# Prologue without GpSimd subtractions, half of the modulation as single columns on TensorE, and a 128-row bias product

## The chip, the cores and the metric

The kernel runs on one core of a Trainium2 chip. The metric is the device time of one execution in microseconds (us), lower is better; the median of three runs before the change is 1759.72 us (1759.67 to 1759.94). Engines are called as the profile calls them: PE (TensorE, the matmuls), PEld (its weight loads), DVE (VectorE), ACT (ScalarE), POOL (GpSimd) and SP (SyncE, which here only issues DMAs).

## The reference

A decoder block on x of 1024 tokens by 1024 channels, in float32. What matters here is its head and one projection:

```python
mod = silu(c) @ w_ada + b_ada              # one row of 6*1024 values
sh1, sc1, g1, sh2, sc2, g2 = split(mod, 6)
h = rms_norm(x, norm_mix_g) * (1.0 + sc1) + sh1
proj = h @ w_in + b_in                     # glu, q/k, v, o, gates, merge
glu_in, qk_in, v, o_pre, if_pre, merge_pre = split(proj)
# a 31-tap causal convolution with GLU beside a chunked mLSTM over q, k, v;
# both merged by sigmoid gates, then w_out, a residual, and a SwiGLU FFN
```

Only sh1 and sc1 (2 x 1024 values, from the first 2048 columns of `w_ada`) are needed before the first projection; the value projection is `v = h @ w_in[:, V] + b_in[V]`.

## The kernel before

Each product of float32 matrices is made of three float32r products: hi x hi, hi x lo and lo x hi, where hi is the value rounded to float32r (written by ACT) and lo is the rest (a subtraction). So each 128-column block of `w_in` needs a load (`wraw`, L140), a hi copy on ACT (L149) and a lo subtraction (L150); then 96 matmuls of 128x512 (L159) over eight 128-channel slices k.

**The prologue** loads x, normalizes its rows (L229 to L238), transposes them on PE into `xT[k]` (L242, evacuated by ACT at L245 or DVE at L247) and computes the modulation. `w_ada` comes as four groups g of 256 channels; a group's tile `wad` holds [128 rows, 8 slices k, 2 halves, 256], half 0 for the shift and half 1 for the scale, and comes by four DMAs (L197). `mod_cols(g)` multiplies each slice by its value of silu(c) and adds it to `macc` on DVE (L266, L268), both halves in one 128x512 instruction. PE then sums `macc` over the partitions with a column of ones (L270, four products of one column) into a one-buffer PSUM tile `pa`; ACT turns these into two columns of `sh1` (L273) and of the gain `G1` (L274). With them ACT writes `hh[k]`, the hi part of h (L304), and h itself over `xT[k]` (L308), and the difference `hl[k]` is a subtraction (L309), for k = 0 and 1 on POOL and else on DVE. `first_products(g)` (L283) is 24 matmuls of 128x512 for the first two blocks of `w_in` (`wf`), whose lo parts POOL subtracts, as it does for the two blocks that come next (`w_next`, POOL at L150, stored as `wlo`). Rows of small parameters (`rows`, L119) are loaded too and transposed by PE into columns (L126, copied by DVE at L129); the first of these holds the bias that ACT needs for its first sigmoid (L364). The first matmul after the prologue is that of L159 in the block of `w_next`.

**Later**, for each of four heads, the value projection (`v_half`, twice) makes four output tiles; each starts with a bias product (L549) of a [64, 128] tile of ones with `b_two`, a [64, 256] tile that is zero but for row 0 (hi of the bias) and row 32 (lo), and 24 matmuls of 128x256 follow (L552 to L554). These are 32 bias products in all.

**What sets the order.** The kernel is written with a tile framework that schedules instructions with its own model of time; each engine then runs its list strictly in the order so found, and waits where a semaphore isn't there yet. DMAs that SP issues take eight semaphores in turn, and each issue after the eighth waits until the DMA that last used its semaphore has landed. `wraw` has two buffers and `pa` has one.

Of the kernel before, what the change touches and what calls it, by code (L numbers as in the profile page):

```python
# [8 lines left out]
F32 = mybir.dt.float32  # L9
F32R = mybir.dt.float32r  # L10
I32 = mybir.dt.int32
AF = mybir.ActivationFunctionType
OP = mybir.AluOpType
# [4 lines left out]
KT = 8  # L18
# [16 lines left out]
AT = (43, 43, 46, 49, 20, 20, 49, 49, 4, 12, 66, 64)  # L35
SCALE = "vvvvvvva"
EVAC = ("aaaaaaaa", "avaavaav")
ON_POOL = (0, 1)
KX = 6
MACC = 3  # L40
XB = 7
# [8 lines left out]
def hybrid_block(ctx: ExitStack, tc: tile.TileContext, x, c, w_ada, b_ada, norm_mix_g, w_in, b_in,  # L50
                 conv_dw_w, conv_dw_b, conv_ln_g, conv_ln_b, w_conv_pw, b_conv_pw, qk_conv_w,
                 qk_conv_b, mlstm_norm_g, w_out, norm_ffn_g, w_ffn_up, w_ffn_down, final_norm_g, out):
    nc = tc.nc
# [5 lines left out]
    const = ctx.enter_context(tc.tile_pool(name="const", bufs=1))  # L59
# [8 lines left out]
    def ps_a():  # L68
        return ps.tile([128, 512], F32, name="pa", bufs=1)

    def ps_n():
        return ps.tile([128, 512], F32, name="pn", bufs=1)

    def ps_c():
        return ps.tile([128, 512], F32, name="pc", bufs=2)
# [20 lines left out]
    ones_col = const.tile([128, 1], F32, name="ones_col")  # L96
    nc.vector.memset(ones_col, 1.0)
    ones_d = const.tile([128, 128], F32, name="ones_d")
    nc.vector.memset(ones_d, 1.0 / D)
    ones_v = const.tile([64, 128], F32R, name="ones_v")  # L100
    nc.vector.memset(ones_v.bitcast(F32), 1.0)
    ones16 = ones_col[0:16, 0:1].to_broadcast([16, 256])

# [3 lines left out]
    def as_rows(ap, n):  # L107
        return bass.AP(tensor=ap.tensor, offset=ap.offset, ap=[[128, n], [1, 128]])
# [3 lines left out]
    def param_rows(group, plan, t=None):  # L112
        if t is None:
            t = pro.tile([128, 128], F32, name=f"rows{group}")
        if sum(n for _, _, n in plan) < 128:
            nc.vector.memset(t, 0.0)
        at = 0
        for key, ap, n in plan:
            nc.sync.dma_start(t[at:at + n, :], ap)  # L119
            at += n  # L120
        return group, plan, t

    def param_columns(rows):
        group, plan, t = rows
        p = ps_a()
        nc.tensor.transpose(p[:, 0:128], t, ident)  # L126
        n = sum(n for _, _, n in plan)
        col = const.tile([128, n], F32, name=f"col{group}")
        nc.vector.tensor_copy(col, p[:, 0:n])  # L129
        at = 0  # L130
        for key, ap, n in plan:
            cols[key] = col[:, at:at + n]
            at += n
# [40 lines left out]
    hh = [big.tile([128, S], F32R, name=f"hh{k}", tag="xa") for k in range(KT)]  # L174

    G1 = const.tile([128, KT], F32, name="G1")
    sh1 = const.tile([128, KT], F32, name="sh1")

    prologue = ExitStack()
    pro = prologue.enter_context(tc.tile_pool(name="pro", bufs=1, reuse_waits="tile"))  # L180
    rows = pro.tile([128, 8, 128], F32, name="rows", tag="macc", bufs=MACC)
    param_columns(param_rows(1, [("c", as_rows(c, 8), 8)], rows[:, 0]))
    sc_c = const.tile([128, KT], F32, name="sc_c")
    nc.scalar.activation(sc_c, cols["c"], AF.Silu)
    xt = []
    for i in range(4):
        t = pro.tile([128, 2, D], F32, name=f"xt{i}")
        nc.sync.dma_start(t, x2[i * 256:(i + 1) * 256, :].rearrange("(a p) d -> p a d", p=128))
        xt += [t[:, 0, :], t[:, 1, :]]
    wad = []  # L190
# [9 lines left out]

    param_columns(param_rows(6, [("b_ada", as_rows(b_ada, 48), 48), ("mix_g", as_rows(norm_mix_g, 8), 8)], rows[:, 1]))
    load_ada(0)
    WF = nc.gpsimd
    WN = nc.gpsimd
    w_first = []
    for i in range(2):
        w_hi, w_lo = (pro.tile([128, KT, 128], F32R, name=f"wf{i}{j}") for j in range(2))
        w_first.append(load_split(win, 0, KT, GLU_B if i == 0 else 0, w_hi, w_lo, eng=WF))
    load_ada(1)
# [16 lines left out]
    for q in range(2):  # L226
# [12 lines left out]
        for k in range(KT):  # L239
            p = ps_n() if k % 3 == 0 else ps_c()  # L240
            for t in range(4):
                nc.tensor.transpose(p[:, t * 128:(t + 1) * 128], xt[q * 4 + t][:, k * 128:(k + 1) * 128], ident)  # L242
            h = xT[k][:, q * 512:(q + 1) * 512]
# [13 lines left out]

    def mod_cols(g):
        p = ps_a()
        part = lambda t, i: t[:, i // 2, (i % 2) * 128:(i % 2) * 128 + 128]  # L260
        b = mod_b[:, g]
        acc = pro.tile([128, 2, 2, 256], F32, name="macc", tag="macc", bufs=MACC)
        for k in range(KT):
            a = acc[:, 0]
            if k < 1:
                nc.vector.tensor_scalar(a, wad[g][:, k], sc_c[:, k:k + 1], None, op0=OP.mult)  # L266
            else:
                nc.vector.scalar_tensor_tensor(a, wad[g][:, k], sc_c[:, k:k + 1], a, op0=OP.mult, op1=OP.add)  # L268
        for i in range(4):
            nc.tensor.matmul(p[:, i:i + 1], part(acc[:, 0], i), ones_col, start=True, stop=True)  # L270
        for i in range(2):
            k = 2 * g + i
            nc.scalar.activation(sh1[:, k:k + 1], p[:, i:i + 1], AF.Identity, bias=b[:, 0, i:i + 1])  # L273
            nc.scalar.activation(G1[:, k:k + 1], p[:, 2 + i:3 + i], AF.Identity, scale=mix_g[:, g, i:i + 1], bias=b[:, 1, i:i + 1])  # L274
# [11 lines left out]
    hl = []  # L286
    for g in range(4):
        mod_cols(g)
        if g == 2:
            rows = pro.tile([128, 8, 128], F32, name="rows", tag="macc", bufs=MACC)  # L290
            later = [
                param_rows(5, [("b_lo", rows_at(b_in, 0, 48), 48), ("b_hi", rows_at(b_in, MC0, 16), 16)], rows[:, 0]),
                param_rows(3, [("dw0", rows_at(conv_dw_w, 0, 128), 128)], rows[:, 1]),
                param_rows(4, [("dw1", rows_at(conv_dw_w, 128 * 128, 120), 120)], rows[:, 2]),
                param_rows(2, [
                    ("dw_b", as_rows(conv_dw_b, 8), 8), ("ln_g", as_rows(conv_ln_g, 8), 8),
                    ("ln_b", as_rows(conv_ln_b, 8), 8), ("pw_b", as_rows(b_conv_pw, 8), 8),
                    ("qk_b", as_rows(qk_conv_b, 16), 16), ("ml_g", as_rows(mlstm_norm_g, 8), 8),
                    ("ffn_g", as_rows(norm_ffn_g, 8), 8), ("qk_w", as_rows(qk_conv_w, 64), 64)], rows[:, 3])]
            bif = const.tile([128, 8], F32, name="bif")  # L300
            nc.sync.dma_start(bif, bass.AP(tensor=b_in.tensor, offset=b_in.offset + IF0, ap=[[0, 128], [1, 8]]))
        ks = (2 * g, 2 * g + 1)
        for k in ks:
            nc.scalar.activation(hh[k], xT[k], AF.Identity, bias=sh1[:, k:k + 1], scale=G1[:, k:k + 1])  # L304
        for k in ks:
            h = xT[k]
            hl.append(big.tile([128, S], F32R, name=f"hl{k}", tag="xb"))
            nc.scalar.activation(h, h, AF.Identity, bias=sh1[:, k:k + 1], scale=G1[:, k:k + 1])  # L308
            (nc.gpsimd if k in ON_POOL else nc.vector).tensor_sub(hl[k], h, hh[k].bitcast(F32))  # L309
        if g > 0:  # L310
            first_products(g - 1)
    first_products(3)
# [9 lines left out]
    hp = hdp.enter_context(tc.tile_pool(name="hp", bufs=1, side="left", reuse_waits="tile"))  # L322
# [47 lines left out]
    def wblock(col0, busy=PUMP, raw=None):  # L370
        w = load_split(win, 0, KT, col0, raw=raw, eng=WN if raw is not None else None)
        acc = ps_mm()
# [143 lines left out]
    def qkv(h):  # L516
# [4 lines left out]
        nc.gpsimd.memset(vl.bitcast(F32)[:, :, 256:258], 0.0)  # L521

        bcols = slice(V0 + h * 256, V0 + h * 256 + 256)
        b_raw, b_hi, b_two = (hp.tile([64, 256], dt, name=n) for n, dt in (("vb_raw", F32), ("vb_hi", F32R), ("vb_two", F32R)))
        nc.gpsimd.memset(b_raw, 0.0)
        for r in (0, 32):
            nc.sync.dma_start(b_raw[r:r + 1, :], b_in[0:1, bcols])
# [34 lines left out]
        q, k = [], []  # L562
# [318 lines left out]
    p = ps_a()  # L881
# [344 lines left out]
    for gidx, nf in enumerate(groups):  # L1226
# [4 lines left out]
        for t in range(8):  # L1231
# [3 lines left out]
            if gidx < 3:  # L1235
                p = ps_mm()
# [40 lines left out]
```

## Time and profile before

| | |
|---|---|
| times of the three runs | 1759.94, 1759.72, 1759.67 us |
| span of the profiled execution | 1757.5 us; its time outside the span isn't on the page, and the runs' median lies 2.2 us above the span |
| PE busy | 1716.9 us, 98% of the span |
| DVE busy | 1253.3 us, 71% |
| ACT busy | 610.9 us, 35% |
| POOL busy | 72.9 us, 4% |
| first matmul after the prologue (L159) | 67.88 us after the span's start |

The span runs from the first instruction to the last. A group's row gives the sum of its instructions' busy time, the mean of one, and how long the engine sat idle just before them. PE's ends are modelled and its matmuls overlap, so on PE the distance from start to start is what an instruction takes of the time, and not its duration.

### The profile page before, as it was taken

The page shows a single profiled execution, that of the slowest core. Times are in us where ns is not written, and L with a number is a line of the kernel's source. Part 1 is how long each engine was busy: PE and PEld are TensorE (multiplying, and loading weights), DVE is VectorE, ACT ScalarE, POOL GpSimd, SP SyncE. Part 2 cuts the span into 40 slices and gives each one's busy share as a digit, 9 for nine tenths or more (in the row PEclk, how much of TensorE's full clock was granted, in tenths as well). Part 3 has the DMA queues.
Part 4 walks back from the last instruction along what each step waited for, and adds up shares of the span by engine and source line. Part 5 has one row for each costly group of instructions (what it writes and reads, how often), then busy time and mean ns, then how long its engine had stood idle before and what let it go on. Part 6 is the DMA issues. An engine that isn't in the chain of part 4 may idle for free.

```text
span 1757.5 us, 21022 instructions
## 1 busy us (share of the span) xinstructions
PE 1716.9 (98%) x8448; PEld 1436.9 (82%) x8448; DVE 1253.3 (71%) x1652; ACT 610.9 (35%) x791; POOL 72.9 (4%) x121
## 2 busy tenths in 40 slices
PE   5999999999999999999999999999999999999998
PEld 4788888888888888888888788888888888878887
DVE  6888998996689858737689567866666665685243
ACT  6434334322533243223522366423222321232122
POOL 3100001000100000000000000000000000000000
PEclk8999999999999999999999999999999999999999
DMA  9121111111111211224497643322222222653221
GB/s 333 33 60 40 46 60 49 49 60 60 49 37 60 62 46 48 73 60 163 136 374 261 204 156 109 108 84 72 84 84 84 72 85 90 221 168 104 64 89 56
DMA packets 194712, 179.93 MB, mean 102 GB/s; under 512 B 7463, under 2 KB 166711, under 8 KB 194615
## 3 DMA queue, kind: packets, MB, share of 16 engines
q1 hardware_dynamic: 177367, 146.61, 26.8%
q10 hardware_dynamic: 17248, 31.99, 5.0%
q8 instruction: 66, 1.08, 0.3%
q14 instruction: 31, 0.25, 0.0%
HBM read 146.06 MB, written 32.51 MB: 102 GB/s over the span
## 4 chain that ended last, share of the span: by engine, by line
PE 90%; DVE 4%; DMA 3%; issue 1%; ACT 1%; POOL 0%; SPq 0%; POOLq 0%; DVEq 0%; ACTq 0%
PE mm L159 39%; PE mm L1054 5%; PE mm L1055 5%; PE mm L1056 4%; PE mm L552 2%; PE mm L1240 2%; PE mm L1239 2%; PE mm L1241 2%; PE mm L553 2%; PE mm L554 2%; PE pc L1054 1%; DVE macc L268 1%; PE pc L1056 1%; PE pc L1055 1%; PE pa L1056 1%
## 5 line engine op out<-in xcount | busy, mean ns | idle before, releaser
L340 DVE SCALAR_TENSOR_TENSOR cacc<-a,col,cacc 128x1024 f32<-128x1024 f32 x240 | 307.3, 1286 | 4.1 <-ACT cacc L338 1.4
L159 PE MATMUL mm<-hh,whi 128*128 128x512 f32 x864 | 272.8, 392 | 0.8 <-ACT t L364 0.8
L159 PE MATMUL mm<-hl,whi 128*128 128x512 f32 x864 | 271.0, 392 | 0.0
L159 PE MATMUL mm<-hh,wlo 128*128 128x512 f32 x864 | 270.6, 391 | 0.0
L159 PEld LDWEIGHTS mm<-hh,whi 128*128 128x128 f32 x864 | 161.1, 188 | 32.8 <-ACT t L364 1.2
L159 PEld LDWEIGHTS mm<-hh,wlo 128*128 128x128 f32 x864 | 161.3, 188 | 32.3
L159 PEld LDWEIGHTS mm<-hl,whi 128*128 128x128 f32 x864 | 160.5, 188 | 30.9 <-issue 0.2
L149 ACT ACTIVATE whi<-wraw 128x1024 fp32r<-128x1024 f32 x62 | 65.8, 1062 | 228.7 <-PE mm L159 178.5
L150 DVE TENSOR_TENSOR wlo<-wraw,whi 128x1024 fp32r<-128x1024 f32 x60 | 73.2, 1220 | 26.1 <-ACT whi L149 26.0
L552 PE MATMUL mm<-whi,hh 128*128 128x256 f32 x256 | 76.2, 298 | 0.0
L1054 PE MATMUL mm<-Bh,gh 128*128 128x512 f32 (+1 forms) x192 | 71.6, 375 | 1.5 <-ACT gh L994 1.0
L553 PE MATMUL mm<-whi,hl 128*128 128x256 f32 x256 | 72.5, 283 | 0.0
L1055 PE MATMUL mm<-Bl,gh 128*128 128x512 f32 (+1 forms) x192 | 71.5, 373 | 0.6 <-DVE Bl L976 0.6
L554 PE MATMUL mm<-wlo,hh 128*128 128x256 f32 x256 | 71.8, 283 | 0.0
L1056 PE MATMUL mm<-Bh,gl 128*128 128x512 f32 (+1 forms) x192 | 71.2, 372 | 0.0
L505 DVE SCALAR_TENSOR_TENSOR cacc<-qkraw,col,cacc 128x1024 f32<-128x1024 f32 x48 | 61.5, 1280 | 6.7 <-ACT cacc L503 6.0
L1243 DVE TENSOR_TENSOR x<-x,mm 128x1024 f32<-128x1024 f32 x24 | 29.3, 1219 | 51.1 <-PE mm L1241 47.0
L1119 ACT ACTIVATE whi<-wraw 128x512 fp32r<-128x512 f32 (+2 forms) x32 | 25.3, 790 | 110.6 <-PE mm L1241 72.9
L552 PEld LDWEIGHTS mm<-whi,hh 128*128 128x128 f32 x256 | 48.8, 191 | 4.1
L1240 PE MATMUL mm<-fa,wlo 128*128 128x512 f32 x128 | 50.1, 392 | 1.0 <-DVE wlo L1120 0.9
L1239 PE MATMUL mm<-fa,whi 128*128 128x512 f32 x128 | 50.0, 390 | 0.9 <-DVE cu L1082 0.9
L1241 PE MATMUL mm<-fa,whi 128*128 128x512 f32 x128 | 49.9, 390 | 0.0
(442 smaller groups left out, 3898.0 us busy)
## 6 DMA issues: line engine op xcount, KB each, us to landing
wraw<-in_w_in_dram SPq DMA_DIRECT2D x64, 512.0 KB, 4.2
awt<-in_w_ada_dram SPq DMA_DIRECT2D x32, 512.0 KB, 8.1
graw<-in_w_ffn_up_dram SPq DMA_DIRECT2D x24, 512.0 KB, 3.8
uraw<-in_w_ffn_up_dram SPq DMA_DIRECT2D x22, 512.0 KB, 4.7
draw<-in_w_ffn_down_dram SPq DMA_DIRECT2D x22, 512.0 KB, 4.4
act_d<-cg ACTq DMA_DIRECT2D x38, 256.0 KB, 2.2
wad<-in_w_ada_dram SPq DMA_DIRECT2D x16, 512.0 KB, 10.2
wraw<-in_w_out_dram SPq DMA_DIRECT2D x16, 512.0 KB, 4.3
```

The costliest lines, as they stand in the source:

```text
L150: (eng or nc.vector).tensor_sub(lo, raw, hi.bitcast(F32))
L159: nc.tensor.matmul(flat(acc)[:, a:b], lhs[:, k, :], rhs[k][:, a:b], start=(first and k == 0), stop=(last and k == kt - 1))
L340: nc.vector.scalar_tensor_tensor(acc, a[:, j:j + S], dw_col(j, ct), acc, op0=OP.mult, op1=OP.add)
L552: nc.tensor.matmul(o, hh[k][:, ts_], hi[:, k % 4, :], start=False, stop=False)
L553: nc.tensor.matmul(o, hl[k][:, ts_], hi[:, k % 4, :], start=False, stop=False)
L554: nc.tensor.matmul(o, hh[k][:, ts_], lo[:, k % 4, :], start=False, stop=(k == KT - 1))
L1054: nc.tensor.matmul(o, a, rh, start=(k == 0), stop=False)
L1055: nc.tensor.matmul(o, a, rl, start=False, stop=False)
L1056: nc.tensor.matmul(o, b, rh, start=False, stop=(k == 3))
L1239: nc.tensor.matmul(o, hi[:, i, :], his[i][:, a:b], start=(i == 0), stop=False)
L1240: nc.tensor.matmul(o, lo[:, i, :], his[i][:, a:b], start=False, stop=False)
L1241: nc.tensor.matmul(o, hi[:, i, :], los[i][:, a:b], start=False, stop=(i == nf - 1))
```

## The change

Five edits, all but the last in the prologue.

1. The four lo subtractions of weights (`wf`, `w_next`) and those of `hl[0]` and `hl[1]` go from POOL to DVE.
2. h (L308) is made by a DVE instruction with two scalars a partition, instead of by ACT.
3. In `mod_cols` DVE accumulates the shift half alone (128x256). The scale half is left to PE: for each 128 columns and each k a product of one column, with the `wad` slice as weights and the column k of silu(c) moving, 16 in a group, adding up in PSUM. The products with ones go from four in a group to two.
4. `macc` is 256 wide instead of 1024, and `rows` has buffers of its own, so that its loads no longer wait for a `macc` buffer.
5. The bias product of the value projection has 128 rows instead of 64; the rows added are zero in `b_two`.

```diff
-WF = nc.gpsimd
-WN = nc.gpsimd
+WF = nc.vector
+WN = nc.vector
...
-        acc = pro.tile([128, 2, 2, 256], F32, name="macc", tag="macc", bufs=MACC)
+        acc = pro.tile([128, 256], F32, name="macc", tag="macc", bufs=MACC)
+        for i in range(2):
+            for k in range(KT):
+                nc.tensor.matmul(p[:, 2 + i:3 + i], wad[g][:, k, 1, i * 128:(i + 1) * 128], sc_c[:, k:k + 1],
+                                 start=(k == 0), stop=(k == KT - 1))
         for k in range(KT):
-            a = acc[:, 0]
             if k < 1:
-                nc.vector.tensor_scalar(a, wad[g][:, k], sc_c[:, k:k + 1], None, op0=OP.mult)
+                nc.vector.tensor_scalar(acc, wad[g][:, k, 0], sc_c[:, k:k + 1], None, op0=OP.mult)
             else:
-                nc.vector.scalar_tensor_tensor(a, wad[g][:, k], sc_c[:, k:k + 1], a, op0=OP.mult, op1=OP.add)
-        for i in range(4):
-            nc.tensor.matmul(p[:, i:i + 1], part(acc[:, 0], i), ones_col, start=True, stop=True)
+                nc.vector.scalar_tensor_tensor(acc, wad[g][:, k, 0], sc_c[:, k:k + 1], acc, op0=OP.mult, op1=OP.add)
+        for i in range(2):
+            nc.tensor.matmul(p[:, i:i + 1], acc[:, i * 128:(i + 1) * 128], ones_col, start=True, stop=True)
...
-            rows = pro.tile([128, 8, 128], F32, name="rows", tag="macc", bufs=MACC)
+            rows = pro.tile([128, 8, 128], F32, name="rows", tag="rows", bufs=2)
...
-            nc.scalar.activation(h, h, AF.Identity, bias=sh1[:, k:k + 1], scale=G1[:, k:k + 1])
-            (nc.gpsimd if k in ON_POOL else nc.vector).tensor_sub(hl[k], h, hh[k].bitcast(F32))
+            nc.vector.tensor_scalar(h, h, G1[:, k:k + 1], sh1[:, k:k + 1], op0=OP.mult, op1=OP.add)
+            nc.vector.tensor_sub(hl[k], h, hh[k].bitcast(F32))
...
-    ones_v = const.tile([64, 128], F32R, name="ones_v")
+    ones_v = const.tile([128, 128], F32R, name="ones_v")
...
-        b_raw, b_hi, b_two = (hp.tile([64, 256], dt, name=n) for n, dt in (("vb_raw", F32), ("vb_hi", F32R), ("vb_two", F32R)))
+        b_raw, b_hi, b_two = (hp.tile([128, 256], dt, name=n) for n, dt in (("vb_raw", F32), ("vb_hi", F32R), ("vb_two", F32R)))
```

The scheduler gives the prologue another order; after the prologue the lists of all engines are the same but for two pairs of neighbours in the FFN. In the lists below the lines of the changed kernel are one lower than before up to `mod_cols` and one higher behind it (L139 is L140 before, L148 is L149, L118 is L119, L274 is L273, L305 is L304, L284 is L283).

SP's list from the last `w_ada` loads on, before:

```order
L197 DMA wad<-in_w_ada_dram 128x4x256 x12
L301 DMA bif<-in_b_in_dram 128x8
L140 DMA wraw<-in_w_in_dram 128x8x128 x2
L119 DMA rows<-in_conv_dw_w_dram 128x128
L119 DMA rows<-in_conv_dw_b_dram 8x128
L119 DMA rows<-in_conv_ln_g_dram 8x128
L119 DMA rows<-in_b_in_dram 48x128
L119 DMA rows<-in_b_in_dram 16x128
```

And after:

```order
L118 DMA rows<-in_conv_dw_w_dram 120x128
L118 DMA rows<-in_conv_dw_b_dram 8x128
L118 DMA rows<-in_conv_ln_g_dram 8x128
L118 DMA rows<-in_conv_ln_b_dram 8x128
L118 DMA rows<-in_b_conv_pw_dram 8x128
L118 DMA rows<-in_qk_conv_b_dram 16x128
L118 DMA rows<-in_mlstm_norm_g_dram 8x128
L118 DMA rows<-in_norm_ffn_g_dram 8x128
L118 DMA rows<-in_qk_conv_w_dram 64x128
L302 DMA bif<-in_b_in_dram 128x8
L139 DMA wraw<-in_w_in_dram 128x8x128 x4
```

The load of `w_next` (the first `wraw` behind the twelve of `wad`) was second behind the last `wad`; now all twelve loads of `rows` and `bif` stand ahead of it, as the 14th.

ACT's list around the modulation of groups 1 and 2, before (hh_84 is `hh[2]`, hh_86 is `hh[4]`):

```order
L308 ACTIVATE xT_157<-xT_157,sh_91,G_90 128x1024
L273 ACTIVATE sh_91<-pa,mod_b 128x1
L274 ACTIVATE G_90<-pa,mod_b,col_117 128x1
L273 ACTIVATE sh_91<-pa,mod_b 128x1
L274 ACTIVATE G_90<-pa,mod_b,col_117 128x1
L304 ACTIVATE hh_84<-xT_158,sh_91,G_90 128x1024
L304 ACTIVATE hh_85<-xT_159,sh_91,G_90 128x1024
```

And after:

```order
L244 ACTIVATE xT_162<-pn 128x512
L148 ACTIVATE whi<-wraw 128x1024
L274 ACTIVATE sh_91<-pa,mod_b 128x1
L275 ACTIVATE G_90<-pa,mod_b,col_117 128x1
L274 ACTIVATE sh_91<-pa,mod_b 128x1
L275 ACTIVATE G_90<-pa,mod_b,col_117 128x1
L148 ACTIVATE whi<-wraw 128x1024
L305 ACTIVATE hh_84<-xT_158,sh_91,G_90 128x1024
L305 ACTIVATE hh_85<-xT_159,sh_91,G_90 128x1024
```

The two hi copies of `w_next` (`whi`) stood behind the modulation of group 2; now the first stands ahead of that of group 1 and the second ahead of `hh[2]`.

PE's list at the end of the first products of group 0 after the change (sc_c moves the column of silu(c); hl_331 is `hl[1]`):

```order
L284 MATMUL mm<-hl_331,wf_124 128x512 x2
L284 MATMUL mm<-hl_331,wf_130 128x512 x2
L263 MATMUL pa<-sc_c,wad 128x1 x16
L271 MATMUL pa<-ones_col,macc 128x1 x2
L284 MATMUL mm<-hh_84,wf_124 128x512 x2
```

Before, four products with ones stood here; now the sixteen single columns of the next group and two products with ones stand between the products of two groups. The four transposes of L126, which were spread among the last products, now stand together behind them, ahead of the first L159.

More of the change, by code (lines that the diff above doesn't have):

```diff
@@ L37 @@
 EVAC = ("aaaaaaaa", "avaavaav")
-ON_POOL = (0, 1)
 KX = 6
@@ L259, in mod_cols @@
         p = ps_a()
-        part = lambda t, i: t[:, i // 2, (i % 2) * 128:(i % 2) * 128 + 128]
         b = mod_b[:, g]
-        acc = pro.tile([128, 2, 2, 256], F32, name="macc", tag="macc", bufs=MACC)
+        acc = pro.tile([128, 256], F32, name="macc", tag="macc", bufs=MACC)
[3 more added lines that the diff above has]
+                                 start=(k == 0), stop=(k == KT - 1))
         for k in range(KT):
-            a = acc[:, 0]
             if k < 1:
-                nc.vector.tensor_scalar(a, wad[g][:, k], sc_c[:, k:k + 1], None, op0=OP.mult)
+                nc.vector.tensor_scalar(acc, wad[g][:, k, 0], sc_c[:, k:k + 1], None, op0=OP.mult)
             else:
-                nc.vector.scalar_tensor_tensor(a, wad[g][:, k], sc_c[:, k:k + 1], a, op0=OP.mult, op1=OP.add)
-        for i in range(4):
-            nc.tensor.matmul(p[:, i:i + 1], part(acc[:, 0], i), ones_col, start=True, stop=True)
+                nc.vector.scalar_tensor_tensor(acc, wad[g][:, k, 0], sc_c[:, k:k + 1], acc, op0=OP.mult, op1=OP.add)
+        for i in range(2):
+            nc.tensor.matmul(p[:, i:i + 1], acc[:, i * 128:(i + 1) * 128], ones_col, start=True, stop=True)
         for i in range(2):
@@ L289, in hybrid_block @@
         if g == 2:
-            rows = pro.tile([128, 8, 128], F32, name="rows", tag="macc", bufs=MACC)
+            rows = pro.tile([128, 8, 128], F32, name="rows", tag="rows", bufs=2)
             later = [
```

## The prediction

> **What bounds the kernel.** First the page, then busy time by stretches, the chain of waits around the end of the prologue, and the queues of that stretch.
>
> ```profile
> PE 1716.9 (98%) x8448; PEld 1436.9 (82%) x8448; DVE 1253.3 (71%) x1652; ACT 610.9 (35%) x791; POOL 72.9 (4%) x121
> 160.00:260.00 100.00, 100.00 (x535) 85.95 (x535) 92.95 (x111) 31.56 (x39) 7.43 (x10) 1.00 0.19 53
> 460.00:560.00 100.00, 100.00 (x560) 86.44 (x559) 85.47 (x92) 36.70 (x39) 2.87 (x5) 1.00 0.17 48
> ...
> 53.23 4.83 PE mm L283 x20
> 66.72 1.12 ACT t L364
> 67.88 22.06 PE mm L159 x96
> ```
>
> From 67.88 us on PE has no gap (columns: stretch, its length, then PE, PEld, DVE, ACT and POOL busy, clock, DMA share, GB/s). So the prologue counts by when that first L159 starts, and later on every TensorE slot saved counts. The sum is made on the profiled execution, whose span is 1757.5 us; the runs' median is 2.2 us longer, and I add the difference to the median.
>
> What DVE did in the prologue, with POOL beside it:
>
> ```profile
> L268 DVE SCALAR_TENSOR_TENSOR macc<-wad,sc_c,macc x28: 635/752/2885, 19.8 to 56.8; 128x512 f32<-128x512 f32 x28
> ```
> ```profile
> 22.81 5.12 POOL L150 TENSOR_TENSOR wf<-wraw,wf 128x1024 fp32r<-128x1024 f32 x2 [5.05 <-ACT wf L149]
> 23.42 2.30 DVE L268 SCALAR_TENSOR_TENSOR macc<-wad,sc_c,macc 128x512 f32<-128x512 f32 x1
> ```
> ```profile
> L268 DVE SCALAR_TENSOR_TENSOR macc<-wad,sc_c,macc 128x512 f32<-128x512 f32 x28 | 32.2, 1154 | 0.6
> L309 DVE TENSOR_TENSOR hl<-xT,hh 128x1024 fp32r<-128x1024 f32 x6 | 7.3, 1221 | 0.7 <-ACT xT L308 0.5
> L238 DVE TENSOR_SCALAR xt<-xt,rstd 128x1024 f32<-128x1024 f32 x7 | 4.8, 750 | 1.6 <-POOL rstd L105 1.6
> ```
>
> **DVE: a gain, but not where the end is set (edits 1 to 4).** The 28 accumulations last 32.2 us where the median of 752 ns gives 21.1: those beside a POOL subtraction stretch to 2.3 or 2.9 us. About 11.1 us of stretching go. Half as wide, an accumulation costs between half of 752 ns and all of it; with the 1221 ns of 1024 elements and 752 of 512 the step is 0.92 ns an element, which gives about 0.5 us, so 28 x 0.25 = 7 us go. There come six subtractions (6 x 1.22 = 7.3) and eight instructions that make h (8 x 0.75 = 6.0 by L238; 9.8 if they run like L309). ACT loses eight of about 1.2 us. Net, DVE is some 5 us lighter. I cost this at nothing: what is late next is neither.
>
> **The load of `w_next` (edit 4, and the new order).**
>
> ```profile
> 32.48 1.80 SPq L197 DMA_DIRECT2D wad<-in_w_ada_dram  x1
> ```
> ```profile
> wad<-in_w_ada_dram SPq DMA_DIRECT2D x2, 512.0 KB, 10.2
> ```
> ```profile
> SPq L119 <- DMA wraw<-in_w_in_dram: 1.3, 1, 1.3
> ```
> ```profile
> 42.60 0.32 SPq L119 DMA_DIRECT2D rows<-in_conv_dw_b_dram  x1
> 42.97 0.29 SPq L119 DMA_DIRECT2D rows<-in_conv_ln_g_dram  x1
> ```
> ```profile
> wraw<-in_w_in_dram SPq DMA_DIRECT2D x6, 512.0 KB, 4.2
> ```
>
> The last `wad` is issued at 32.48 and lands 10.2 us later, at 42.7. A load of `rows`, which shares no tile with `wraw`, waited 1.3 us for one: that is the semaphore of the DMA eight issues earlier. After the change the eighth issue behind the last `wad` is the eighth of the loads of `rows` (that of the pointwise bias), so it goes at 42.7; then three more `rows`, the one of `qk_conv_w`, `bif` and only then `w_next`: six issues of 0.37 to 0.5 us, so 45.1. It lands 4.2 us later, at 49.3. Before, `w_next` was issued at 35.85 and was there when ACT came to it at 47.78:
>
> ```profile
> 35.85 0.37 SPq L140 DMA_DIRECT2D wraw<-in_w_in_dram  x1
> ```
> ```profile
> 47.78 1.07 ACT L149 ACTIVATE whi<-wraw 128x1024 fp32r<-128x1024 f32 x1
> ```
>
> ACT now has the hi copy of that load ahead of the modulation of group 1, which before ran at 39.8, and all behind it waits: hh of groups 1 to 3, and through the one-buffer `pa` PE's single columns of group 2, which may not overwrite group 1's.
>
> ```profile
> 39.77 0.26 ACT L273 ACTIVATE sh<-pa,mod_b 128x1 f32<-128x1 f32 x1 [3.12 <-PE pa L270]
> 40.55 2.38 ACT L304 ACTIVATE hh<-xT,sh,G 128x1024 fp32r<-128x1024 f32 x2
> 50.99 1.06 ACT L149 ACTIVATE whi<-wraw 128x1024 fp32r<-128x1024 f32 x1
> 51.94 2.37 ACT L308 ACTIVATE xT<-xT,sh,G 128x1024 f32<-128x1024 f32 x2
> ```
> ```profile
> 29.20:31.30 2.10, 1.87 (x8) 1.78 (x8) 0.50 1.09 348
> 57.60:58.90 1.30, 0.95 (x8) 1.05 (x8) 1.00 1.19 300
> ```
> ```profile
> 62.15 0.27 PE L126 MATMUL pa<-ident,rows 128*128 128x128 f32 x1
> 62.45 0.28 DVE L129 COPY col<-pa 128x120 f32<-128x120 f32 x1 [0.75 <-PE pa L126]
> ```
>
> The hi copy takes 0.95 us of ACT (50.99 to 51.94), the four small modulation steps 0.78 (39.77 to 40.55): 49.3 + 1.7 = 51.0. From there PE alone is the chain. Four products with ones last 0.95 us with overlap, 0.85 from start to start, 0.21 for each of one column (rows above; eight records for four, since a float32 product is two passes). The single columns are the same form, so 16 + 2 of them take 3.8 us; 24 matmuls of L283 take 24 x 22.06/96 = 5.5 us. Behind 51.0 stand columns 2, products 1, columns 3, products 2 and 3: 2 x 3.8 + 3 x 5.5 = 24.1, so 75.1. Then four transposes, each waiting until DVE has copied the one ahead out of `pa` (0.27 + 0.28 and about 0.1 between them): 2.6, beside which ACT's sigmoid (1.12) fits. L159 starts at 77.7 instead of 67.88: **+9.8 us**. DVE's h and hl for a group (2 x 0.75 + 2 x 1.22 = 3.9 us) are shorter than PE's 9.3 a group.
>
> **The clock of PE.**
>
> ```profile
> 33.31 5.64 PE L283 MATMUL mm<-hh,wf 128*128 128x512 f32 x16 [2.12 <-ACT hh L304]
> 45.91 1.05 PE L270 MATMUL pa<-ones_col,macc 128*128 128x1 f32 x8 [2.65 <-DVE macc L268]
> ```
> ```profile
> 47.30:50.60 3.30, 3.30 (x10) 2.55 (x9) 3.26 (x4) 3.30 (x6) 1.67 (x1) 0.50 0.06 15
> ```
>
> PE ran at half clock for 3.3 us here, after a wait of 2.65 us. After the change PE is through with group 0 at about 43 (its products began at 33.3 before; the 3.8 us of group 1's columns now stand ahead of them, and they take 5.5) and waits 8 us. Then at least one such stretch at half clock costs 1.7 us. Single columns keep the array hardly busy, so they may not count as work: then columns 2 run wholly at half clock (+3.8), the products behind them for another 3.3 to 6.6 us (+1.7 to 3.3), and columns 3 may start it again (+1.7). Bounds 1.7 and 9; I take 3.5, columns 2 about wholly at half clock, as the row of 29.20 shows them (1.87 for 0.95), because that is sure by the length of the wait. By the Trainium skill, "TensorE: Matmul & The Clock Gate", section "What's actually happening", one idle window of 3.4 us throttles and one busy window releases, which would be 1.7 to 3.4 us here; it does not say what a column counts.
>
> **The bias product (edit 5).**
>
> ```profile
> 159.32 0.28 PE L553 MATMUL mm<-whi,hl 128*128 128x256 f32 x1
> 159.44 0.28 PE L554 MATMUL mm<-wlo,hh 128*128 128x256 f32 x1
> 159.65 0.38 PE L549 MATMUL mm<-vb_two,ones_v 64*128 64x256 f32 x1
> 159.95 0.38 PE L552 MATMUL mm<-whi,hh 128*128 128x256 f32 x1
> 160.18 0.28 PE L553 MATMUL mm<-whi,hl 128*128 128x256 f32 x1
> 160.29 0.28 PE L554 MATMUL mm<-wlo,hh 128*128 128x256 f32 x1
> ```
> ```profile
> 159.64 0.18 PEld L549 LDWEIGHTS mm<-vb_two,ones_v 64*128 64x128 f32 x1
> 159.95 0.19 PEld L552 LDWEIGHTS mm<-whi,hh 128*128 128x128 f32 x1
> ```
> ```profile
> L549 PE MATMUL mm<-vb_two,ones_v x32: 378/380/383, 142.0 to 681.8; 64*128 64x256 f32 x32
> ```
>
> From start to start the 128-row matmuls take 0.12 us (159.32 to 159.44). Around the 64-row one it is 0.21, 0.30 and 0.23: 0.74 where three would take 0.36, so 0.38 lost. Its weights load at 159.64, with it and not ahead of it, and those of the next matmul too: the overlap of load and matmul breaks on both sides of the 64-row tile. With 128 rows it is of its neighbours' form. 32 x 0.38 = **-12.2 us**. Bounds: 0, if the break comes from the tile of ones, and 13, if more goes; I take 12.2, since 64*128 is what sets it apart from its neighbours. DVE is 93% busy from 160 to 260, so it may take back 1 or 2 us. The wider memset and copies of the bias tiles lie off PE.
>
> The Trainium skill speaks against this gain: "TensorE: Matmul & The Clock Gate", section "LDWEIGHTS (loading the stationary operand)", has the load go by columns and not by rows ("it's the 128 columns that matter"). The durations agree, 0.18 and 0.19 us; the distances of the starts do not. "TensorEngine Tiling (Array Packing)", section "Key Properties", has a change of tiling mode drain the engine, which is what the distances look like. By the first page edit 5 gives 0 and the sum is 1773.0; by the second it is as forecast.
>
> **Sum.** 9.8 + 3.5 - 12.2 = +1.1 us: 1759.72 + 1.1 = 1760.8.
>
> **Rivals.**
> - The padding gains nothing, as the duration of 0.18 us of the load would have it: 1759.72 + 13.3 = 1773.0, slower. Against it stand the six distances above. It turns slower by over 0.2% if less than 0.30 us of the 0.38 go. Chance 0.06.
> - Single columns don't count as work for the clock, so half clock costs 9 instead of 3.5: 1766.3, slower. For it: a column moves one value a row for 128 loaded; against it: nothing shown. It decides from about 6 us on. Chance 0.21 (0.19 slower, 0.02 the same).
> - The load of `w_next` isn't late (its issue gets through by 36, or lands sooner): then PE goes on from group 0 at 43 with 24.1 + 2.6 us: 69.7, +1.8 and no half clock: 1749.3, faster. Against it stands the wait of 1.3 us above; for it only that the 4.2 us landing might shrink behind small loads. It is faster by over 0.2% once the load lands before 45. Chance 0.10.
>
> **How the numbers follow.** The forecast case, loss and gain nearly cancelling, has 0.60 and a range of its own of 1756.5 to 1764.5 (half clock 1.7 to 5, landing 48.5 to 50.5, gain 11 to 13). About 0.2% (3.5 us) is what a measurement of this kernel can tell from no change: 1756.2 to 1763.2. Of the 0.60 some 0.48 lie within it, 0.05 below and 0.07 above. With the rivals, and 0.03 for a gain that I don't see: faster 0.05 + 0.10 + 0.03, 0.18; same 0.48 + 0.02, 0.50; slower 0.07 + 0.06 + 0.19, 0.32. The range is 1754 to 1767: it leaves out the first rival and most of the third.
>
> **What would show it.** On ACT the first `whi` waits for the DMA until about 49, with an idle of some 9 us ahead of it; columns 2 start at about 51; granted clock 0.50 between 47 and 58; L159 starts at 78 to 84; L268 has no instruction above 1 us; the bias products and the next matmuls start 0.12 us apart. It is wrong if `w_next` lands before 47, if the clock stays at half beyond 60, or if the distance at the bias product stays at 0.3.

## The result, and the profile after

| | kernel before | changed kernel |
|---|---|---|
| median of the runs | 1759.94 us (1759.67 to 1762.36, 7 runs) | 1766.66 us (1764.11 to 1768.92, 7 runs) |
| span of the profiled execution | 1757.5 us | 1764.9 us |
| first L159 (L158 after) behind the prologue, the start of the main products | 67.88 us | 85.69 us |

The changed kernel is slower by 6.7 us: its time is 1.0036 times that of before, 95% interval 1.0025 to 1.0046. The forecast was 1760.8 us in a range of 1754 to 1767. The profiled executions differ by 7.4 us, and I account for these.

From the page of the changed kernel, then its busy time in a stretch that is shown of before, and what was the `macc` line L268 (duration of one: min/median/max in ns):

```profile
PE 1722.7 (98%) x8560; PEld 1452.0 (82%) x8560; DVE 1247.5 (71%) x1666; ACT 602.0 (34%) x783; POOL 56.4 (3%) x115
```
```profile
160.00:260.00 100.00, 100.00 (x587) 88.28 (x586) 94.53 (x120) 34.49 (x43) 4.72 (x6) 1.00 0.19 54
```
```profile
L269 DVE SCALAR_TENSOR_TENSOR macc<-wad,sc_c,macc x28: 474/485/486, 16.2 to 43.6; 128x256 f32<-128x256 f32 x28
```

DVE has indeed lost its stretched accumulations (0.49 us at most, where up to 2.9 stood), and from 160 us on PE is as full as before (587 matmuls where 535 stood don't mean more work done: this trace runs some 17 us late there, so the window holds another piece of the program). The time is lost ahead of that. The timeline of SP's queue and of ACT, and PE's waits and timeline in the prologue (start, length, engine, line, operation, count; in brackets the idle time ahead and what ended it):

```profile
45.29 8.98 SPq L139 DMA_DIRECT2D wraw<-in_w_in_dram  x4
```
```profile
49.83 1.06 ACT L148 ACTIVATE whi<-wraw 128x1024 fp32r<-128x1024 f32 x1 [13.45 <-DMA wraw<-in_w_in_dram]
50.79 0.24 ACT L274 ACTIVATE sh<-pa,mod_b 128x1 f32<-128x1 f32 x1
```
```profile
PE pa L263 <- ACT G L275: 8.0, 1, 8.0
```
```profile
41.72 1.98 PE L284 MATMUL mm<-hl,wf 128*128 128x512 f32 x8
51.73 6.99 PE L263 MATMUL pa<-sc_c,wad 128*128 128x1 f32 x32 [8.04 <-ACT G L275]
58.58 0.99 PE L271 MATMUL pa<-ones_col,macc 128*128 128x1 f32 x4
59.43 6.00 PE L284 MATMUL mm<-hh,wf 128*128 128x512 f32 x16
65.27 1.98 PE L284 MATMUL mm<-hl,wf 128*128 128x512 f32 x8
67.08 3.63 PE L263 MATMUL pa<-sc_c,wad 128*128 128x1 f32 x32
70.57 0.85 PE L271 MATMUL pa<-ones_col,macc 128*128 128x1 f32 x4
71.28 5.23 PE L284 MATMUL mm<-hh,wf 128*128 128x512 f32 x16
...
83.60 0.27 PE L125 MATMUL pa<-ident,rows 128*128 128x128 f32 x1
...
85.69 0.71 PE L158 MATMUL mm<-hh,whi 128*128 128x512 f32 x2
```

The chain is the one that was forecast: the load of `w_next` lands late, ACT's hi copy waits for it with group 1's modulation behind it, and PE, done with group 0 at 43.7, waits 8.04 us in front of the columns of group 2. Now the granted clock of the same time (columns: stretch, length, then PE, PEld, DVE, ACT and POOL busy with instructions, clock, DMA share, GB/s):

```profile
46.90:51.70 4.80, 0.00 (x0) 0.00 (x0) 0.78 (x1) 1.87 (x6) 0.00 (x0) 0.50 0.79 214
51.70:59.40 7.70, 7.67 (x36) 7.67 (x37) 5.57 (x6) 3.17 (x3) 0.00 (x0) 0.50 0.60 140
59.50:63.80 4.30, 4.30 (x11) 3.38 (x11) 2.10 (x3) 3.15 (x6) 0.00 (x0) 0.50 0.01 2
64.00:70.60 6.60, 6.60 (x48) 6.03 (x46) 1.69 (x2) 0.00 (x0) 0.00 (x0) 1.00 0.00 0
70.80:74.10 3.30, 3.30 (x11) 2.72 (x11) 0.58 (x1) 2.64 (x6) 0.00 (x0) 0.50 0.00 0
74.20:83.50 9.30, 9.30 (x42) 7.69 (x42) 3.31 (x4) 1.69 (x2) 0.00 (x0) 1.00 0.00 0
```

Read the second and the fourth row together. From 51.7 on PE is busy without a gap (x32 is 16 products of one column, two passes each), yet the clock stays at half until 63.9: all through the columns and 4.5 us into the products behind them. At 70.7, after a stretch in which PE was busy 6.60 of 6.60 us, it falls to half again: columns 3 had begun at 67.08. From the first column at 51.73 to the transposes at 83.60 PE takes 31.9 us, where the prediction had 24.1 at full clock.

The bias product, timeline of PE from 178.4 us on:

```profile
178.42 0.28 PE L550 MATMUL mm<-vb_two,ones_v 128*128 128x256 f32 x1
178.54 0.28 PE L553 MATMUL mm<-whi,hh 128*128 128x256 f32 x1
178.66 0.28 PE L554 MATMUL mm<-whi,hl 128*128 128x256 f32 x1
```

All starts are 0.12 us apart. **The sum of the profiled executions**, from the starts of the same matmuls in both traces: 17.8 us late at the start of the main products, 5.75 late at 700 us (12.06 gained on 32 products), 6.8 late from 1115 us on and 7.4 from 1596 us on. The last 1.7 us are several waits of PE that are each some tenths longer; I did not trace them further.

### The profile page after: what moved, and what is told of

It reads as the page before. It is cut to its first block, busy times and chain, and to the rows that moved or that the text cites. A ratio compares the mean times of both kernels' runs of the same rounds, so it can differ in the third digit from the quotient of the medians.

```text
span 1764.9 us, 21240 instructions
## 1 busy us (share of the span) xinstructions
PE 1722.7 (98%) x8560; PEld 1452.0 (82%) x8560; DVE 1247.5 (71%) x1666; ACT 602.0 (34%) x783; POOL 56.4 (3%) x115
## 3 DMA queue, kind: packets, MB, share of 16 engines
q1 hardware_dynamic: 177367, 146.61, 26.8%
## 4 chain that ended last, share of the span: by engine, by line
PE 91%; DMA 4%; DVE 2%; SPq 1%; issue 1%; ACT 1%; POOLq 0%; POOL 0%; DVEq 0%; ACTq 0%
PE mm L158 39%; PE mm L1055 5%; PE mm L1056 4%; PE mm L1057 4%; PE mm L1240 2%; PE mm L1241 2%; PE mm L1242 2%; PE mm L553 2%; PE mm L554 2%; PE mm L555 2%; PE pc L1055 1%; PE pc L1057 1%; PE pc L1056 1%; PE mm L284 1%; PE pa L1057 1%; PE pa L1056 1%
## 5 line engine op out<-in xcount | busy, mean ns | idle before, releaser
L158 PE MATMUL mm<-hh,whi 128*128 128x512 f32 x864 | 272.6, 392 | 0.0
L158 PE MATMUL mm<-hl,whi 128*128 128x512 f32 x864 | 270.8, 391 | 0.0
L158 PE MATMUL mm<-hh,wlo 128*128 128x512 f32 x864 | 270.4, 391 | 0.0
L158 PEld LDWEIGHTS mm<-hh,wlo 128*128 128x128 f32 x864 | 161.2, 188 | 32.4
L158 PEld LDWEIGHTS mm<-hh,whi 128*128 128x128 f32 x864 | 161.1, 188 | 31.7 <-issue 0.2
L158 PEld LDWEIGHTS mm<-hl,whi 128*128 128x128 f32 x864 | 160.3, 188 | 31.0 <-issue 0.2
L148 ACT ACTIVATE whi<-wraw 128x1024 fp32r<-128x1024 f32 x62 | 65.8, 1061 | 245.4 <-PE mm L158 180.2
L149 DVE TENSOR_TENSOR wlo<-wraw,whi 128x1024 fp32r<-128x1024 f32 x62 | 75.6, 1220 | 31.6 <-ACT whi L148 31.4
L1244 DVE TENSOR_TENSOR x<-x,mm 128x1024 f32<-128x1024 f32 x24 | 29.2, 1218 | 52.3 <-PE mm L1242 49.6
```

What stands on the lines that cost most here:

```text
L149: (eng or nc.vector).tensor_sub(lo, raw, hi.bitcast(F32))
L158: nc.tensor.matmul(flat(acc)[:, a:b], lhs[:, k, :], rhs[k][:, a:b], start=(first and k == 0), stop=(last and k == kt - 1))
```

## The experiments

Theory A was the forecast's: the late load, and a half clock that comes with the wait. Theory B, its second rival: single columns do not count as work for the clock, so they bring half clock by themselves. Beside them stood the question whether the padding, and nothing else, makes the 12 us. Each ratio is to the kernel before, run on the same chip; the experiments ran on several chips, so between two of them the ratios and their 95% intervals are what compares. The start of the main products is read from the profiled execution, the time is the median of the runs.

**1. The padding alone** (`pad_alone`), in the kernel before:

```diff
-    ones_v = const.tile([64, 128], F32R, name="ones_v")
+    ones_v = const.tile([128, 128], F32R, name="ones_v")
-        b_raw, b_hi, b_two = (hp.tile([64, 256], dt, name=n) ...
+        b_raw, b_hi, b_two = (hp.tile([128, 256], dt, name=n) ...
```

> The kernel before with only the padding of the bias product. Forecast theory (each of the 32 products loses 0.38 us because its tile has 64 rows among tiles of 128): 12.1 us faster than before, about 1747.8 us; the starts around the product become 0.12 us apart, and the end of the prologue stays at 67.9 us. Rival (the 12 us seen after the change come from the lighter DVE and ACT, not from the rows): no change within 2 us, starts still 0.21, 0.30 and 0.23 us apart. A smaller gain of 8 to 10 us would say that DVE, 93% busy from 160 to 260 us, takes some of it back.

Measured: 1748.51 us, ratio 0.9931 (0.9919 to 0.9943), some 12 us faster. Between the start of the main products (68.06 us, 0.18 later than before) and 876 us the trace gains 11.99 us. The forecast theory holds, and the lighter DVE of the changed kernel had no part in it. Behind 980 us this execution gives back 1.5 us.

**2. The padding undone** (`undo_pad`) in the changed kernel (the same lines the other way round).

> The changed kernel with the bias product back at 64 rows; the new prologue stays. Forecast theory: 12.1 us slower than the changed kernel, 1778.7 us, that is 19 us slower than before, of which 17.8 us lie ahead of the first matmul of the main products. Rival (the padding plays no part): 1766.7 us as the changed kernel.

Measured: 1778.32 us, ratio 1.0101 (1.0088 to 1.0114), 11.7 us above the changed kernel. From 68 to 970 us of before's time this trace stands 19.1 us late, without change. The timeline of PE shows the 64-row tile with 0.21, 0.31 and 0.23 from start to start, as in the kernel before:

```profile
178.50 0.28 PE L555 MATMUL mm<-wlo,hh 128*128 128x256 f32 x1
178.71 0.38 PE L550 MATMUL mm<-vb_two,ones_v 64*128 64x256 f32 x1
179.02 0.38 PE L553 MATMUL mm<-whi,hh 128*128 128x256 f32 x1
179.25 0.28 PE L554 MATMUL mm<-whi,hl 128*128 128x256 f32 x1
```

So the two halves of the change add up: the padding is worth 12 us with either prologue, and the prologue alone costs 18 to 19.

**3. The weight loads first** (`loads_first`). The rows get their old buffers back, which makes their loads wait and lets those of `w_next` go ahead (the first pair of lines stands twice in the kernel):

```diff
-    rows = pro.tile([128, 8, 128], F32, name="rows", tag="rows", bufs=2)
+    rows = pro.tile([128, 8, 128], F32, name="rows", tag="macc", bufs=MACC)
-        acc = pro.tile([128, 256], F32, name="macc", tag="macc", bufs=MACC)
+        acc = pro.tile([128, 4, 256], F32, name="macc", tag="macc", bufs=MACC)[:, 0]
```

> The changed kernel with one difference: the parameter rows share the buffers of the accumulators again, so that both next weight loads are issued ahead of the rows. The order of ACT and of PE behind group 0 stays. Theory A (the late load holds ACT, and through the one-buffer pa PE): the load is issued at about 36 us and lands at about 43, PE's wait ahead of the columns of group 2 shrinks from 8.0 to about 1.5 us, and with no wait of 3.4 us the clock stays at full there; main products start at about 72 to 75 us instead of 85.7, the kernel takes 1753 to 1756 us. Theory B (single columns do not count as work, so the columns bring half clock by themselves): the wait shrinks as in A, but columns 2 still start a stretch at half clock, and columns 3 too, each costing 1.5 to 3 us: main products at 76 to 79 us, 1756 to 1760 us. Theory C (the wait is not the load's): 1766.7 us, no change.

Measured: 1761.74 us, ratio 1.0005 (0.9996 to 1.0014), 4.9 us faster than the changed kernel; main products at 81.2 us. The hi copy starts at 44.69 instead of 49.83 and PE's wait is 2.86 us. Timeline of PE, then stretches:

```profile
46.58 6.79 PE L263 MATMUL pa<-sc_c,wad 128*128 128x1 f32 x32 [2.86 <-ACT G L275]
...
61.03 4.22 PE L263 MATMUL pa<-sc_c,wad 128*128 128x1 f32 x32
```
```profile
46.90:57.00 10.10, 10.10 (x42) 9.52 (x42) 8.66 (x14) 5.56 (x9) 0.53 (x1) 0.50 0.50 115
57.10:63.80 6.70, 6.70 (x44) 5.98 (x43) 3.21 (x4) 0.32 (x1) 0.00 (x0) 1.00 0.00 0
63.90:70.70 6.80, 6.80 (x22) 5.83 (x23) 2.47 (x3) 4.44 (x7) 0.00 (x0) 0.50 0.00 0
```

The late load is real but worth only about 5 us. The half clock stays: 10.2 us from 46.8 on, and 6.8 us from 63.9 on, right behind columns 3, ahead of which PE had not waited at all. The first of the two still comes with the wait, though at 2.86 us that is shorter than the 3.4 that theory A asked for: the fall at 46.8 lies 0.2 us behind the start of the columns. The second is B in kind; in size even B's 76 to 79 us was too low.

**4. Wide columns** (`columns_wide`). The same sums, with the scaling vector repeated, so that each weight tile multiplies 64 columns instead of one:

```diff
-                nc.tensor.matmul(p[:, 2 + i:3 + i], wad[g][:, k, 1, ...], sc_c[:, k:k + 1],
+                nc.tensor.matmul(p[:, 128 + 64 * i:128 + 64 * (i + 1)], wad[g][:, k, 1, ...], sc_c[:, k:k + 1].to_broadcast([128, 64]),
```

> The changed kernel with each single column computed 64 times over (the same weights, the scaling vector repeated 64 times as moving data; 64 equal columns are written and the first is used). The late load and PE's wait of 8 us stay. Theory B (a column moves too little data to count as work): with 64 columns the half clock that begins in the wait ends 3.4 to 7 us after columns 2 begin, that is by 59 us instead of 63.9, and no second half-clock stretch follows columns 3 at 70.7; the wide columns last at most a little longer at full clock (3.6 us a group before); main products start 4 to 6 us earlier, about 80 us, unless the wide columns cost more. Rival (half clock comes from the wait alone and lasts as long whatever PE does next): half clock to 63.9 us as before, and the second stretch too; no gain.

Measured: 1752.75 us, ratio 0.9959 (0.9948 to 0.9971), 14 us faster than the changed kernel; main products at 76.8 us. The profiled execution was the slowest of the six (1758.49 us), so the trace shows less gain than the median has. And the scheduler, which reckons with longer columns, had also put group 1's modulation ahead of the waiting hi copy, so this is more than the one difference. Against the expectation a half clock that began with a wait of 4.3 us lasted 13.7 us in it, from 52.9 to 66.5. Hence the next one.

**5. Wide columns in a kept order** (`wide_locked`): as 4, but built on loads_first and for groups 2 and 3 alone, which leaves the order of PE and ACT as it was up to the last products.

> The kernel of loads_first, with the columns of groups 2 and 3 alone computed 64 times over (same weights, the scaling vector repeated as moving data); the order of PE and ACT is that of loads_first up to the last products. In loads_first the clock was half from 46.82 to 57.06 and, with no wait ahead of columns 3, again from 63.89 to 70.71. Theory B (single columns do not count as work for the clock): with 64 columns the second stretch does not come (columns 3 at full clock, about 3.6 to 3.8 us), and the first ends after one or two of its 3.4 us windows, at 50.2 or 53.7; main products at about 75.5 to 78 us instead of 81.2, the kernel 3 to 5 us faster than loads_first, about 1757 to 1759 us. Rival (the stretches come from waits, not from what the columns do): both stretches stay, 1761.7 us as loads_first, or slower by what wider columns cost.

Measured: 1758.27 us, ratio 0.9980 (0.9970 to 0.9990), 3.5 us faster than loads_first (4.4 by the ratios); main products at 77.4 us.

```profile
47.20:57.30 10.10, 10.10 (x40) 9.33 (x40) 9.07 (x14) 5.49 (x9) 0.52 (x1) 0.50 0.50 114
57.40:64.30 6.90, 6.90 (x48) 6.27 (x46) 2.31 (x3) 0.00 (x0) 0.00 (x0) 1.00 0.00 0
64.40:74.00 9.60, 9.60 (x47) 7.94 (x46) 4.12 (x5) 4.45 (x7) 0.00 (x0) 1.00 0.00 0
```

The second stretch at half clock is gone, as B says: columns 3, with the same weights, hold the clock at full when they move 64 columns and lose it when they move one. The first stretch is as long as before, against B's 3.4 to 7 us: 64 columns keep the clock up but did not bring it back.

**6. Twice as wide** (`wide128_locked`), 128 columns, otherwise as 5.

> As wide_locked, with the columns of groups 2 and 3 computed 128 times over instead of 64 (same order up to the last products). In wide_locked the stretch after columns 3 was gone, but the one that the wait began lasted three windows (47.13 to 57.37), through the wide columns of group 2. If what releases the clock is a fuller window, twice the moving data releases it one or two windows earlier, by 50.5 or 54, and main products start at 73 to 77 us (77.4 in wide_locked), less what the wider columns themselves cost: a column of 64 took 0.115 us at full clock, and if 128 take 0.2 the group costs 2.7 us more. If it takes products to release it, the stretch stays until 57 and the kernel is slower than wide_locked by what the columns cost, 0 to 6 us.

Measured: 1757.48 us, ratio 0.9982 (0.9972 to 0.9991), level with wide_locked. On the question it was made for it is inconclusive: in its profiled execution PE ran slower earlier, group 0 ended only at 49.6, and there was no wait to be released from. The single columns of groups 0 and 1 lasted 0.21 us each there, half speed, from 21.8 us on; the clock's records of this execution begin only at 45.4. What it does show is that 128 columns cost hardly more than one, 32 passes in 3.73 us, with the clock at full from 45.4 us into the main products.

**7. Two buffers for the sums** (`two_buffers`): loads_first, with the sums in the two-buffer tile `pc` instead of the one-buffer `pa`, so PE need not wait for ACT.

```diff
     def mod_cols(g):
-        p = ps_a()
+        p = ps_c()
```

> The kernel of loads_first with the modulation's sums in the two-buffer tile of the transposes instead of the one-buffer pa, so PE's columns need not wait for ACT to have read the group ahead; ACT's hi copies of the next weights now stand behind group 1's modulation. Theory B: every group's columns are 3.6 us and more of PE time that does not count as work, so a stretch at half clock still follows at least one of them: main products at 72 to 77 us, 1752 to 1757 us. Theory A (it is the waits that cost): the clock is full from 47 us on, main products at about 70 us, 1750 us.

Measured: 1759.64 us, ratio 0.9988 (0.9979 to 0.9997); main products at 75.6 us, as B had it. The time misses B's 1752 to 1757 us: at 876 us this execution stands 4.4 us ahead of the kernel before, and behind 980 it gives back 4.7.

```profile
26.30:31.10 4.80, 4.80 (x45) 4.80 (x44) 4.11 (x9) 1.19 (x5) 0.00 (x0) 1.00 1.10 349
31.20:41.40 10.20, 10.20 (x40) 9.33 (x40) 7.56 (x15) 5.61 (x9) 0.00 (x0) 0.50 1.10 343
41.50:48.20 6.70, 6.70 (x47) 6.10 (x46) 6.65 (x10) 2.11 (x2) 0.00 (x0) 1.00 0.63 150
48.30:55.00 6.70, 6.70 (x19) 5.44 (x19) 5.48 (x7) 3.15 (x6) 0.53 (x1) 0.50 0.72 171
55.10:61.80 6.70, 6.70 (x49) 6.19 (x49) 0.28 (x1) 0.25 (x2) 0.00 (x0) 1.00 0.00 0
62.00:65.20 3.20, 3.20 (x9) 2.52 (x8) 1.55 (x2) 2.71 (x5) 0.00 (x0) 0.50 0.00 0
```

This is the clearest row of the study: PE has no gap from 26.3 to 65.2 us, and three times, behind each batch of single columns, its clock goes to half, for 20.5 us in all. Theory A, which had the clock full from 47 us on without a wait, falls as the whole account.

**8. Two buffers and wide columns** (`two_buffers_wide`): as 7, with all columns 64 wide.

> The kernel of two_buffers with the columns of all groups computed 64 times over (order changed at few places: some columns of group 2 move up between the products of group 0). Theory B: nothing in the prologue is then idle work for the clock from group 0's columns on, so the 20.5 us at half clock that two_buffers had between 31 and 65 us (10.24, 6.83 and 3.41) shrink to 7 or less, main products start at 66 to 70 us instead of 75.6, and the kernel takes 1746 to 1751 us, level with the kernel before with padding alone (1748.5) or ahead of it. Rival (the stretches are waits'): no change against two_buffers, 1759.6 us.

Measured: 1748.45 us, ratio 0.9931 (0.9917 to 0.9945), 10 to 11 us faster than two_buffers. Stretches, and the timeline of PE:

```profile
25.90:33.50 7.60, 7.60 (x70) 7.60 (x69) 6.79 (x16) 3.75 (x7) 0.00 (x0) 1.00 1.09 349
33.60:43.00 9.40, 9.40 (x61) 8.39 (x60) 7.78 (x12) 3.16 (x6) 0.00 (x0) 1.00 1.12 333
43.10:49.00 5.90, 5.90 (x30) 4.99 (x30) 5.27 (x9) 4.45 (x8) 0.52 (x1) 1.00 0.41 95
49.00:65.00 16.00, 15.61 (x88) 13.19 (x86) 8.93 (x12) 6.14 (x9) 0.25 (x2) 1.00 0.31 70
```
```profile
49.03 3.68 PE L263 MATMUL pc<-sc_c,wad 128*128 128x64 f32 x32
...
65.62 0.71 PE L158 MATMUL mm<-hh,whi 128*128 128x512 f32 x2
```

The clock is full throughout, 32 passes of 64 columns take 3.68 us against 3.63 for 32 of a single one, and the main products start at 65.6 us, 10 us earlier than with single columns and 2.3 us earlier than in the kernel before. They start just ahead of the expected 66 to 70 us, and the time lies within the expected 1746 to 1751. Between 876 us and the end this execution gives back 4.8 us (14.1 ahead of before, then 9.2), and so it ends level with the padding alone. One part of that is the clock, at half for 6.83 us from 982 on where the kernel before has 3.41 us; the rest I did not trace.

**9. No columns** (`no_columns`): loads_first, with DVE making both halves of the modulation again and 32 products with ones, as before; subtractions and h stay on DVE.

> The changed kernel without the single columns: DVE makes both halves of the modulation as before, 32 products with ones do the sums; the subtractions stay on DVE, h stays on DVE, the rows' loads stand behind the next weights' as before, and the padding stays. Theory (the columns, by their own time on PE and by the half clock that they bring, are what the prologue lost): main products start at 65 to 69 us, the kernel takes 1745 to 1750 us, as the kernel before with padding alone (1748.5) or better. Rival (DVE, now with the subtractions, h and full-width accumulations, becomes the bound): main products at 73 us or later, 1753 us or more.

Measured: 1751.87 us, ratio 0.9942 (0.9929 to 0.9954); main products at 71.0 us, between the two expectations. Against loads_first 10 to 11 us are gained, so the columns and their half clock were most of the loss. Half clock is not theirs alone, though: here it begins within PE's waits, at 31.83 us (until 38.65) and again at 45.48, in the longest of them, 4.76 us, which ends at 46.85:

```profile
45.50:52.20 6.70, 5.35 (x13) 4.19 (x14) 6.50 (x8) 3.38 (x4) 0.00 (x0) 0.50 0.36 97
```

Against the padding alone 2 to 3 us are lost (the intervals of the two ratios overlap, but the main products start 2.9 us later). The waits of PE from 20 to 75 us show where:

```profile
PE mm L282 <- ACT hh L303: 7.2, 4, 4.8
PE pa L269 <- DVE macc L267: 2.7, 1, 2.7
```

It is not the DVE that the rival named, but mostly ACT, whose hi copy of `w_next` still stands ahead of group 1's hh (start 44.61, after 2.72 us of waiting for the load).

**10. No columns, two buffers** (`no_columns_two_buffers`): as 9, with the sums in `pc`.

> The kernel of no_columns with the sums in the two-buffer tile, so neither PE nor ACT waits for the other's use of pa. If ACT's wait for the next weight load (about 44.7 us) and pa are what is left in the prologue, main products start at 63 to 67 us and the kernel takes 1743 to 1748 us, 1 to 4 us faster than no_columns. If DVE is the bound there, no change against no_columns.

Measured: 1752.07 us, ratio 0.9944 (0.9931 to 0.9956): no change, and the expectation missed. `pa` was not what held it. In this trace the waits of PE read:

```profile
PE pa L125 <- DMA rows<-in_b_in_dram: 5.0, 1, 5.0
PE mm L282 <- ACT hh L303: 3.2, 2, 2.1
```

The freed `pa` let a transpose of the rows move up between group 0 and group 1, and PE now waits for its load where it had waited for ACT. It says nothing on DVE.

The best two, the padding alone (1748.51) and two buffers with wide columns (1748.45), both beat the kernel before and the changed kernel. They are level: the intervals of their ratios are the same within 0.0002.

## Why the prediction came out as it did

The time fell into the range near its upper end, at the place of the second rival (1766.3, chance 0.21) and not of the likeliest case, whose own range of 1756.5 to 1764.5 it missed. The stated range holds because it was drawn over that rival too; the mechanism of the likeliest case holds for the load and the bias product and not for the clock.

- **Late load: right.** Issue forecast 45.1 and seen 45.3; landing 49.3, and the hi copy began at 49.83; columns 2 forecast at 51.0, seen at 51.73. The 0.7 us are a late landing and a longer small chain. The 9 us of idle ahead of the hi copy were 13.45, since ACT had finished its earlier work sooner, which costs nothing. The "+9.8 us" held to within 0.2 us: 0.7 more here, 0.5 less on the transposes (2.1 instead of 2.6).
- **Half clock: mis-sized, and this is the step that failed.** The term was 3.5 us; it measured 7.8 (31.9 us of PE where 24.1 stood). Of that the columns of group 2 with their ones take 3.9 (7.7 for 3.8, as foreseen), products 1 take 2.15 (7.65 for 5.5), columns 3 some 0.4, and products 2 and 3 some 1.3 from the second stretch. The mistake was to price what the wait makes sure and to leave the rest to a rival: the clock was taken to come back once PE is busy. Experiments 3, 5, 7 and 8 show that a PE busy with single columns does not bring it back, and even loses it. The prediction named "stays at half beyond 60" as what would prove it wrong, and it stayed until 63.9; the main products, expected at 78 to 84, started at 85.69. The trace of before already held a longer case than the 3.3 us that the forecast priced: its clock was at half from 26.8 to 37.0 us, three times 3.41, though PE was busy 7.88 of the 10 us from 30 on:

```profile
30.00:40.00 10.00, 7.88 (x32) 6.65 (x33) 9.79 (x13) 5.64 (x10) 4.33 (x2) 0.65 1.09 349
```

- **Bias product: right.** 12.2 forecast; 12.06 seen in the changed kernel, 11.99 in the padding alone; all starts 0.12 apart. The first rival (no gain) falls by experiments 1 and 2. The rule behind it, the Trainium skill's "it's the 128 columns that matter" ("TensorE: Matmul & The Clock Gate", section "LDWEIGHTS (loading the stationary operand)"), agrees with the load's own duration, 0.18 us for 64 rows and 0.19 for 128, but not with the slot, and the measurement decides. The drain on a change of mode in "TensorEngine Tiling (Array Packing)", section "Key Properties", agrees with the distances; if it is such a drain, its price here is 0.38 us for one tile.
- **DVE and ACT at nothing: right.** Behind group 0 PE waits for DVE only at the copies of the transposes, 1.1 us in three waits, and the rest of its waiting there is ACT's 8.0: what DVE was spared does not show in the time.
- **The third rival** (the load is not late) is answered by experiment 3: even with the loads first the kernel takes 1761.7 us and not 1749.3, because its price left out the wait that stays (2.86 us, with half clock behind it) and the half clock that single columns bring.

In sum: 17.8 late instead of 13.3, 12.06 back instead of 12.2, and 1.7 us lost behind 990 us that no step had. There a reading of the prediction was wrong: from 67.88 us on PE has no gap in the stretches shown, but behind 990 us it waits again, in the kernel before for 3.5 us at once, with 3.41 us at half clock behind it, and at ten more places for 0.3 to 1.0 us:

```profile
PE pa L946 <- ACT whi L940: 3.5, 1, 3.5
```

The phase of the clock's changes is not fixed. In the profiled executions the first fall lies at 26.4 us (changed kernel), 32.5 (padding undone) and 31.2 (two buffers), and later changes lie whole multiples of 3.41 us behind it: 10.24, 6.83, 17.07. The Trainium skill, "TensorE: Matmul & The Clock Gate", section "What's actually happening", has a free-running window of about 3.4 us, and the trace agrees. Where such a window falls decides how many of them a batch of columns fills, which may be why the kernels with single columns spread over 5 to 8 us (1764.1 to 1768.9, 1757.4 to 1765.3) and the padding alone over 1.5; that is argued, not shown. Against it stand columns_wide, whose modulation columns are all 64 wide and which yet spreads from 1751.0 to 1758.5, and the mean clocks of single runs of loads_first, 0.992 in the fastest (1757.4 us) and 0.996 in the slowest (1765.3), though the clock's records can begin late, as in experiment 6.

## What to carry to other kernels

Matmuls with one moving column counted as idle time for the clock, however full the timeline showed PE: a batch of 3.6 us either ran at half clock or left the clock at half for the products behind it. Waits do the same: one of 2.86 us was enough. If such columns are needed, repeat the moving operand (32 passes of 64 columns took 3.68 us where single ones took 3.63), and look at the granted clock, not at the busy time. And a tile of odd shape among uniform ones is priced by the distances of the starts around it: its own duration (0.38 for 0.28 us) shows 0.10 of the 0.38 us that it cost.

## What the runs showed of the hardware beyond that

- Keeping and regaining the clock differ. At full clock, 64-wide columns held it (experiments 5 and 8); at half clock, two windows of 3.41 us mostly filled with them did not bring it back (47.1 to 54.0 us in wide_locked). 512-wide products brought it back where they filled 84 or 87% of a window (70.74 to 74.15 in the changed kernel, products from 71.28; 53.65 to 57.06 in loads_first, products from 54.09) and not where they filled 75 or 82% (48.24 to 51.66 in two_buffers, products from 49.09; 31.83 to 35.24 in no_columns, products from 32.44). But they are not the only work that does: at 36.6 us of the changed kernel and of loads_first the clock came back after a window without one, most of it transposes of 128 columns (in the changed kernel from 33.37 to 35.96 of 33.19 to 36.61). What share of which work is needed either way stays open.
- A float32 matmul of 128 moving columns takes nearly the PE slot of one of a single column when each needs new weights: 32 passes in 3.73 us against 3.63.
